# A decoder step: rows gathered without their norm, the factor gathered per slot, the last output product in two pieces, two subtractions on GpSimd

## The chip, the cores and the metric

One core of a Trainium2 chip runs the whole step. The metric is the device time of one launch in microseconds. The kernel before takes 429.27 us (median of 3 runs, 428.23 to 430.04).

## The reference

One layer of a decoder with 256 prompt tokens (two tiles of 128 rows, called 0 and 1) and 8 new tokens (tile 2, 8 rows), 1024 wide. What matters here comes after the attention:

```
hres = x + concat([att, conv_y]) @ w_out                 # output product
hn   = hres * rsqrt(mean(hres**2) + eps) * g_ffn         # second norm
lg, le = hn @ w_rg + b_rg, hn @ w_re + b_re              # 4 group logits, 32 expert logits
g    = argmax(lg);  two best experts inside group g, weights by softmax
h    = silu(hn @ w_gate[e]) * (hn @ w_up[e]) * gate
y    = hres + sum over the two experts of h @ w_down[e]; then a last norm
```

There are 32 experts with three 1 MB weights each in float32, so 96 MB of weights pass through the core whatever the tokens choose.

## The kernel before, in words

The work up to the expert groups is a list of named steps written out by hand (ORDER). Each engine (TensorE, VectorE, ScalarE, GpSimd) and SyncE's DMA queue takes its instructions in the order in which these steps issue them, so a step that waits holds back everything behind it on its engine.

For tile t the steps are: `o..` the output product with its add into yres; `H` per half of 512 columns the sum of squares on ScalarE, four transposes and their scaled copy xh; `l` the logits; `R` the norm's factor, whose power is taken on GpSimd (line 824); `L` the logits with the factor and bias; `N` the normed row rounded to the short float format, hn, on ScalarE (line 833); `O` what the rounding left, hlo, on VectorE (line 839). Products of the short format run faster, and hn and hlo together keep the precision. `ra` to `re` are the routing on VectorE (lines 872 to 912): best group, best and second expert, the choice matrix A, and the gates G. `rk` ranks a token among those of its expert by a matmul with A (lines 922, 923), `oh` makes of the rank the one-hot matrix Pg (line 938).

Tokens are gathered by matmuls with Pg: 32 slots for each of 4 experts, so 128 slots in a group (`g..`, line 949: hn and then hlo, for tiles 0, 2 and 1). The rows are copied out of PSUM (`gr`, line 958), transposed and scaled by g_ffn into xg (`gt`, lines 965, 966). `warm0` and `warm1` are matmuls whose result is not used (line 288). Then follow 8 groups: gate product pgt and hidden product pup (line 1085), silu (1146), the slot maps (1066 to 1075), the multiplication of the two (1155), the gather for the next group, the down product pyy (1099), and the combine back into yres (1116, 1190).

Weights go through a ring of 15 buffers of 1 MB and some free halves and quarters, filled from SP's queue in a fixed order. A load waits until the buffer's last reader is done. The buffers of the output weights take part in it: the last gate weight of group 1 waits for the last output product. Where the ring is full ahead of the groups, the next load waits for the gate product of group 0.

Of the kernel before, what the change touches and what calls it, by code (L numbers as in the profile page):

```python
# [19 lines left out]
D = 1024  # L20
NTOK = 256
NB = 8
H = 8
# [10 lines left out]
FILL = 4  # L34
# [52 lines left out]
def hymba_step(ctx: ExitStack, tc: tile.TileContext, x_prompt, x_sample, cache_k, cache_v, state_conv,  # L87
# [35 lines left out]
    with tc.manual_schedule():  # L123
# [626 lines left out]
        def out_mm(t, n, kk):  # L750
            if kk == 0:
                accs["o", t, n] = ps("py", "acc")
            po = accs["o", t, n]
            for c in range(4 * kk, 4 * kk + 4):
                T.matmul(po, lhsT=mixT[:, c, 128 * t:128 * t + 128], rhs=wo[n, c // 4][:, c % 4, :],  # L755
                         start=c == 0, stop=c == 7)
            if kk == 1:
                yv = yres[:, t, 512 * n:512 * n + 512]
                V.tensor_tensor(yv, yv, po, op=OP.add)
# [16 lines left out]
        for n in range(2):  # L776
            for t in range(2):
                for kk in range(2):
                    steps[f"o{t}{n}{kk}"] = lambda t=t, n=n, kk=kk: out_mm(t, n, kk)
            steps[f"z{n}"] = lambda n=n: out_quad(n)  # L780
            steps[f"y{n}"] = lambda n=n: out_sum(n)
# [6 lines left out]
        def norm2_half(t, hf):  # L788

            n = NR[t]  # L790
            if hf == 0:
# [5 lines left out]
                else:  # L797
                    hlo[t] = c4(f"hlo{t}", [128, 8, 128], F32R)
                ss2[t] = c1(f"ssb{t}", [128, 2])
                xh[t] = c4("xh", [128, 8, 128])  # L800
            y = yres[:n, t, 512 * hf:512 * hf + 512]
            S.activation(hlo[t][:n, 4 * hf:4 * hf + 4, :].rearrange("t c p -> t (c p)"), y, AF.Square,
                         accum_out=ss2[t][:n, hf:hf + 1])
            pt = ps("pt")
            pv_ = pt.rearrange("p (c n) -> p c n", c=4)
            for c in range(4):
                T.transpose(pv_[:, c, 0:n], y[:, 128 * c:128 * c + 128], ident[:n, :n])
            x = xh[t][:, 4 * hf:4 * hf + 4, 0:n]
            V.tensor_tensor(x, pv_[:, :, 0:n], gfT[:, 4 * hf:4 * hf + 4, None].to_broadcast([128, 4, n]), op=OP.mult)

        def norm2_log(t, hf):
            n = NR[t]
            if hf == 0:
                PL[t] = ps("pl", "acc")
            for c in range(4 * hf, 4 * hf + 4):
                T.matmul(PL[t][:n, 0:36], lhsT=xh[t][:, c, 0:n], rhs=wr[:, c, :], start=c == 0, stop=c == 7)

        def norm2_rs(t):
            n = NR[t]
            r = c1(f"rs{t}", [128, 1])  # L820
            rs2[t] = small(f"rsb{t}", [128, 1])
            V.tensor_tensor(r[:n], ss2[t][:n, 0:1], ss2[t][:n, 1:2], op=OP.add)
            V.tensor_scalar(r[:n], r[:n], 1.0 / D, EPS, op0=OP.mult, op1=OP.add)
            P.tensor_tensor(rs2[t][:n], r[:n], mhalf[:n], op=OP.pow)
# [6 lines left out]
        def norm2_hn(t):  # L831
            n = NR[t]
            S.activation(hn[t][:n].rearrange("t c p -> t p c"), yres[:n, t, :].rearrange("t (p c) -> t p c", c=8),
                         AF.Copy, scale=rs2[t][:n])

        def norm2_lo(t):

            n = NR[t]
            V.scalar_tensor_tensor(hlo[t][:n], yres[:n, t, :].rearrange("t (p c) -> t c p", c=8), rs2[t][:n],
                                   hn[t][:n].bitcast(F32), op0=OP.mult, op1=OP.subtract)  # L840

        for t in range(3):
            for hf in range(2):
                steps[f"H{t}{hf}"] = lambda t=t, hf=hf: norm2_half(t, hf)
                steps[f"l{t}{hf}"] = lambda t=t, hf=hf: norm2_log(t, hf)
            steps[f"R{t}"] = lambda t=t: norm2_rs(t)
            steps[f"L{t}"] = lambda t=t: norm2_L(t)
# [493 lines left out]
```

## Time and profile before

| what | us |
|---|---|
| runs before, median (lowest to highest) | 429.27 (428.23 to 430.04) |
| profiled execution, its own time | 429.14 |
| its span, first to last instruction | 427.1 |
| TensorE, VectorE, ScalarE, GpSimd busy | 377.5, 198.0, 90.6, 101.2 |
| data moved | 155.02 MB, mean 363 GB/s |

Busy shares are means over stages with different limits. The page cuts the span into 40 slices of 10.7 us; the timeline lists instructions with start, duration, engine, line, output and inputs, and in brackets what the engine had waited for. TensorE's clock has two levels; PEclk is the granted share of full speed.

### The profile page before, as it was taken

Reading aid. Unit: us, or ns where it says so; the run is one execution under the profiler, and the core shown is the slowest. Engines: PE = TensorE matmul, PEld = TensorE weight load, DVE = VectorE, ACT = ScalarE, POOL = GpSimd, SP = SyncE. Lnnn points to the kernel's source line nnn. Section 1 sums busy time; section 2 is a strip of 40 time slices with the busy share of each in tenths; the row PEclk is TensorE's granted clock in tenths of the full one; section 3 lists DMA queues with packets and bytes.
Section 4 is the critical chain, followed back from the end, with each engine's and each line's share of the span. In section 5 each row is a group of like instructions: output and inputs, shape, how many; then the busy total and the mean of one; then the engine's idle time right before and its main releaser. Section 6 shows DMA issues by size and latency. Waiting matters only on the chain.

```text
span 427.1 us, 6429 instructions
## 1 busy us (share of the span) xinstructions
PE 377.5 (88%) x2574; PEld 201.5 (47%) x2574; DVE 198.0 (46%) x383; ACT 90.6 (21%) x214; POOL 101.2 (24%) x101
## 2 busy tenths in 40 slices
PE   7899999899999999987989898979679689788981
PEld 6354355578775334345545444434334344343630
DVE  1257987899774024577424242405005106024045
ACT  4221223164330003332311121102002012011023
POOL 3627888978205001000000000000000000000022
PEclk9999999999999999985799999999969989799996
DMA  7999986869988999949299999999999999999953
GB/s 266 398 360 411 365 348 243 344 224 409 418 329 306 421 423 418 409 186 371 68 413 397 424 418 424 417 423 421 417 424 420 421 422 417 424 420 413 393 185 104
DMA packets 32979, 155.02 MB, mean 363 GB/s; under 512 B 3068, under 2 KB 5322, under 8 KB 17972
## 3 DMA queue, kind: packets, MB, share of 16 engines
q1 hardware_dynamic: 27328, 119.69, 70.1%
q0 software_dynamic: 5008, 33.80, 20.2%
q10 hardware_dynamic: 612, 1.11, 0.7%
q8 instruction: 21, 0.34, 0.3%
q14 instruction: 10, 0.08, 0.1%
HBM read 152.40 MB, written 2.20 MB: 362 GB/s over the span
## 4 chain that ended last, share of the span: by engine, by line
PE 38%; DMA 34%; DVE 12%; issue 8%; POOL 6%; ACT 1%; DVEq 0%; POOLq 0%; SPq 0%; ACTq 0%
DMA g<-in_w_gate_dram 10%; DMA u<-in_w_up_dram 9%; DMA d<-in_w_down_dram 9%; PE py L755 7%; DMA K<-in_cache_k_dram,idx 5%; PE pyy L1099 4%; PE pgt L1085 3%; PE pov L710 3%; DVE Sd L481 3%; PE accB L553 3%; PE px L949 3%; PE pup L1085 3%; POOL K L475 2%; POOL K L304 2%; PE warm L288 2%
## 5 line engine op out<-in xcount | busy, mean ns | idle before, releaser
L1085 PE MATMUL pup<-u,xg 128*32 128x256 f32 x472 | 40.6, 442 | 12.8 <-DMA u<-in_w_up_dram 12.7
L1062 POOL TENSOR_TENSOR PGw<-Pg,G 128x384 f32<-128x384 f32 x8 | 6.7, 834 | 177.1 <-DVE Pg L938 134.4
L1155 DVE TENSOR_TENSOR sh<-pup,sh 128x256 f32<-128x256 f32 x8 | 4.8, 603 | 91.3 <-PE pup L1085 84.2
L475 POOL TENSOR_TENSOR K<-K,qv 128x2048 f32<-128x2048 f32 x9 | 40.7, 4540 | 4.7 <-DMA K<-in_cache_k_dram,idx 3.1
L481 DVE TENSOR_REDUCE Sd<-K 128x32 f32<-128x2048 f32 x16 | 35.9, 2277 | 6.0 <-POOL K L475 5.9
L1085 PE MATMUL pgt<-g,xg 128*32 128x256 f32 x512 | 31.8, 384 | 3.6 <-DMA g<-in_w_gate_dram 3.6
L1085 PEld LDWEIGHTS pup<-u,xg 128*32 128x32 f32 x472 | 18.5, 126 | 31.1 <-DMA u<-in_w_up_dram 17.0
L949 PE MATMUL px<-hn,Pg 128*128 128x512 f32 (+1 forms) x48 | 23.0, 504 | 11.2 <-DVE Pg L938 11.2
L1099 PE MATMUL pyy<-d,hT 128*32 128x512 f32 (+1 forms) x272 | 30.7, 570 | 0.6 <-DVE hT L1176 0.6
L755 PE MATMUL py<-wo,mixT 128*128 128x512 f32 x64 | 30.2, 622 | 0.0
L1116 PE MATMUL pz<-Y,PT 128*128 128x512 f32 (+1 forms) x90 | 26.5, 421 | 0.7
L958 ACT COPY xr<-px 128x512 f32<-128x512 f32 x16 | 9.3, 587 | 83.1 <-PE px L949 83.1
L1190 DVE TENSOR_TENSOR yres<-yres,pz 128x512 f32<-128x512 f32 (+1 forms) x42 | 25.6, 670 | 0.0
L1085 PEld LDWEIGHTS pgt<-g,xg 128*32 128x32 f32 x512 | 16.3, 111 | 18.2 <-DMA g<-in_w_gate_dram 5.2
L1108 DVE SCALAR_TENSOR_TENSOR Y<-pyy,gsl,Y 128x512 fp32r<-128x512 f32 (+1 forms) x17 | 12.2, 719 | 25.3 <-ACT Y L1107 25.3
L1107 ACT ACTIVATE Y<-pyy,gsl 128x512 fp32r<-128x512 f32 (+1 forms) x17 | 11.3, 663 | 43.9 <-PE pyy L1099 43.9
L1116 PEld LDWEIGHTS pz<-Y,PT 128*128 128x128 f32 (+1 forms) x90 | 12.1, 154 | 17.9 <-ACT Y L1107 6.4
L949 PEld LDWEIGHTS px<-hn,Pg 128*128 128x128 f32 (+1 forms) x48 | 9.2, 195 | 23.8 <-DVE Pg L938 11.7
L304 POOL DMA_INDIRECT V<-in_cache_v_dram,idx x16 | 15.1, 947 | 22.1 <-PE pov L710 18.2
L755 PEld LDWEIGHTS py<-wo,mixT 128*128 128x128 f32 x64 | 12.3, 199 | 14.3 <-issue 14.1
L304 POOL DMA_INDIRECT K<-in_cache_k_dram,idx x16 | 15.6, 973 | 14.6 <-DMA K<-in_cache_k_dram,idx 7.8
L477 DVE TENSOR_TENSOR K<-K,qb 128x2048 f32<-128x2048 f32 x7 | 16.0, 2280 | 2.2 <-DMA K<-in_cache_k_dram,idx 2.2
(325 smaller groups left out, 595.2 us busy)
## 6 DMA issues: line engine op xcount, KB each, us to landing
g<-in_w_gate_dram SPq DMA_DIRECT2D x32, 1024.0 KB, 19.9
d<-in_w_down_dram SPq DMA_DIRECT2D x28, 1024.0 KB, 19.8
u<-in_w_up_dram SPq DMA_DIRECT2D x25, 1024.0 KB, 19.8
u<-in_w_up_dram SPq DMA_DIRECT2D x9, 512.0 KB, 14.5
wo<-in_w_out_dram SPq DMA_DIRECT2D x4, 1024.0 KB, 16.3
wk<-in_w_in_dram SPq DMA_DIRECT2D x2, 1024.0 KB
wv<-in_w_in_dram SPq DMA_DIRECT2D x2, 1024.0 KB, 32.2
wC<-in_w_in_dram SPq DMA_DIRECT2D x2, 1024.0 KB
```

The costliest lines, as they stand in the source:

```text
L304: P.indirect_dma_start(out=t, out_offset=None, in_=src, in_offset=bass.IndirectOffsetOnAxis(ap=idx[:, b, hh:hh + 1], axis=0))
L475: P.tensor_tensor(kslots[i], kslots[i], qv[:, None, :].to_broadcast([128, 4, 512]), op=OP.mult)
L477: V.tensor_tensor(kslots[i], kslots[i], qbs[b][:, None, :].to_broadcast([128, 4, 512]), op=OP.mult)
L481: V.tensor_reduce(Sd[:, b, 4 * hh:4 * hh + 4, :].rearrange("p i h -> p (i h)"), kslots[i].rearrange("p i (h d) -> p (i h) d", h=8), axis=A ...
L553: T.matmul(acc[:, 0:264], lhsT=W[pn, kk][:, c, 128 * m:128 * m + 128], rhs=xnT[:, cc, 0:264], start=cc == 0, stop=cc == 7)
L710: T.matmul(po[32 * j:32 * j + 32], lhsT=pvs[b // 4][:, b % 4, i, :], rhs=vslots[2 * b + i // 4][:, i % 4, :], start=s == 0, stop=s == 1, t ...
L755: T.matmul(po, lhsT=mixT[:, c, 128 * t:128 * t + 128], rhs=wo[n, c // 4][:, c % 4, :], start=c == 0, stop=c == 7)
L949: T.matmul(PX[grp, hf], lhsT=PgS[grp][:n, POS[t]].rearrange("p j s -> p (j s)"), rhs=(hn, hlo)[low][t][:n, 4 * hf:4 * hf + 4, :].rearrange ...
L1085: T.matmul(dst[32 * j:32 * j + 32, 0:256], lhsT=xg[:, c, 32 * j:32 * j + 32], rhs=w[:, 256 * k:256 * k + 256], start=c == 0, stop=c == 7, ...
L1099: T.matmul(py[32 * j:32 * j + 32, 0:w], lhsT=hT[:, c, 32 * j:32 * j + 32], rhs=dw[grp, j][:, 1024 * c + a:1024 * c + b], start=c == 0, sto ...
L1116: T.matmul(pz, lhsT=PTS[grp][:, 128 * t:128 * t + NR[t]], rhs=Y[:, i, 0:w], start=start and i == 0, stop=i == 1, skip_group_check=more)
L1190: V.tensor_tensor(yv, yv, pz[:m], op=OP.add)
```

## The change

- hn is now the rounded row without its norm, made per column piece right after the piece's add (in `H`), and hlo (`O`) the plain difference. Tile 1's second half is cut in two pieces of 256 columns. Tile 2's two `O` pieces are on GpSimd.
- The norm's factor is gathered per slot by three matmuls (`gather_rs`), and enters silu's scale and the multiplication of silu with pup. For group 0 this stands behind the gate products, for the other groups behind the gather of the rows.
- The last output product (tile 1, second half) is issued as two pieces of 256 columns with an add each.
- The routing takes the two best experts with MAX over 8 columns instead of two rounds of reductions.
- The part of tile 1's rank that needs only the other tiles is issued ahead (`rk1p`). Fillers are three times two matmuls of 256 columns instead of twice four of 128.
- The row copies of group 0 are shared by ScalarE and VectorE, as is the scaling into xg.
- In the groups the next group's Pg stands ahead of the multiplication of silu with pup.

```diff
-o001 V6 H00 G31 o011 V7 H01 X1 pe l00 o100 R0 l01 L0 ra0 rb0 rc0 o101 as rk0 N0 co rd0 z0 z1 y0 oh0 H10 y1 H20
-O0 H21 l20 R2 g00 re0 l21 L2 ra2 rb2 room o111 l10 N2 rc2 H11 O2 R1 g01 rk2 oh2 N1 rd2 l11 L1 ra1 rb1 rc1 g20 warm0 g21
-warm1 rk1 oh1 O1 g10h g11h re2 g10l gr0 g11l gr1 gt0 gt1 rd1 re1
+o001 V6 H00 G31 o011 V7 H01 X1 pe l00 o100 R0 l01 L0 ra0 rb0 O00 rc0 o101 as rk0 O01 co rd0 z0 z1 y0 oh0 H10 y1 H20
+H21 l20 R2 g00 O20 l21 O21 L2 ra2 rb2 room g01 o111 rc2 l10 O10 o112 H11 R1p H12 rk2 oh2 R1 O11 l11 l12 L1 ra1 rb1 rc1
+g20 warm0 g21 warm1 rk1p rk1 warm2 oh1 O12 rd2 g10h g11h re0 g10l ga0 g11l ga1 re2 gt0 gt1 rd1 re1
...
+        COLS = {0: ((0, 512), (512, 512)), 2: ((0, 512), (512, 512)), 1: ((0, 512), (512, 256), (768, 256))}
...
+            S.copy(hn[t][:n, :, p].rearrange("t c p -> t p c"), y.rearrange("t (p c) -> t p c", c=8))
+        def norm2_lo(t, k):
+            n = NR[t]
+            a, w = COLS[t][k]
+            p = slice(a // 8, (a + w) // 8)
+            (P if t == 2 else V).tensor_tensor(
+                hlo[t][:n, :, p], yres[:n, t, a:a + w].rearrange("t (p c) -> t c p", c=8),
+                hn[t][:n, :, p].bitcast(F32), op=OP.subtract)
...
+            V.scalar_tensor_tensor(r[:n, 1:2], ss2[t][:n, m:m + 1], 1.0 / D, r[:n, 0:1], op0=OP.mult, op1=OP.add)
+            P.tensor_tensor(rs2[t][:n], r[:n, 1:2], mhalf[:n], op=OP.pow)
...
+            V.max(e8, l8)
+            e1, e2 = e8[:, 0:1], e8[:, 1:2]
+            V.scalar_tensor_tensor(f, l8, e2, w8, op0=OP.is_ge, op1=OP.mult)
             yield
+            V.tensor_scalar(g8, l8, e2, 8.0, op0=OP.is_gt, op1=OP.mult)
+            V.tensor_tensor(f, f, g8, op=OP.add)
+            V.max(p8, f)
+            m1, m2 = p8[:, 0:1], p8[:, 1:2]
+            V.tensor_scalar(a8, f, m2, None, op0=OP.is_ge)
...
+            w = 256 if grp == 0 else 512
+            S.copy(rows_[:, 0:w], px[:, 0:w])
+            if w < 512:
+                V.tensor_copy(rows_[:, w:512], px[:, w:512])
+        def gather_rs(grp):
+            prs = ps("prs", "acc")
+            for t in range(3):
+                n = NR[t]
+                T.matmul(prs[:, 0:1], lhsT=fl(PgS[grp], t, n).bitcast(F32), rhs=rs2[t][:n], start=t == 0, stop=t == 2)
+            RSl[grp] = wp.tile([128, 1], F32, name="rsl", tag="rsl", bufs=2)
+            S.copy(RSl[grp], prs[:, 0:1])
...
+            m = 2 if grp == 0 else 4
+            V.tensor_tensor(XG[grp][:, 4 * hf:4 * hf + m, :], pt[:, 0:m, :],
+                            gffT[:, 4 * hf:4 * hf + m, None].to_broadcast([128, m, 128]), op=OP.mult)
+            for c in range(m, 4):
+                cc = 4 * hf + c
+                S.activation(XG[grp][:, cc, :], pt[:, c, :], AF.Copy, scale=gffT[:, cc:cc + 1])
...
             mm_exp(pgt, gw, grp)
+            if grp == 0:
+                gather_rs(0)
-            S.activation(sg, pgt[:, 0:256], AF.Silu)
+            S.activation(sg, pgt[:, 0:256], AF.Silu, scale=RSl[grp])
...
             mm_exp(pup, uw, grp)
+            if grp < LAST:
+                onehot(grp + 1)
+            V.scalar_tensor_tensor(hh_.rearrange("s c p -> s p c"), pup[:, 0:256].rearrange("s (p c) -> s p c", c=2),
+                                   RSl[grp], sg.rearrange("s (p c) -> s p c", c=2), op0=OP.mult, op1=OP.mult)
```

## Rows read from the trace of the kernel before

**Rows 1.** The page's slices: what all DMA engines moved, GB/s, per slice.
```profile
GB/s 266 398 360 411 365 348 243 344 224 409 418 329 306 421 423 418 409 186 371 68 413 397 424 418 424 417 423 421 417 424 420 421 422 417 424 420 413 393 185 104
```

**Rows 2.** The chain of waits: start, duration in us, what held the end.
```profile
271.41 19.81 DMA d<-in_w_down_dram
...
392.15 3.64 PE pgt L1085 x58
```

**Rows 3.** Windows: length, busy us per engine (instructions), granted clock, DMA share, GB/s.
```profile
185.50:190.00 4.50, 4.50 (x15) 2.27 (x14) 2.17 (x10) 0.90 (x1) 0.00 (x0) 0.81 0.02 7
190.50:203.80 13.30, 9.39 (x40) 6.70 (x39) 10.56 (x38) 2.68 (x6) 0.62 (x2) 0.63 0.95 352
194.00:207.50 13.50, 10.74 (x41) 7.33 (x45) 9.32 (x38) 3.29 (x6) 0.62 (x2) 0.50 0.71 266
204.00:212.00 8.00, 7.75 (x82) 4.49 (x80) 3.84 (x18) 3.51 (x8) 0.83 (x1) 0.77 0.01 3
226.00:228.00 2.00, 1.91 (x9) 0.94 (x7) 1.55 (x3) 0.41 (x1) 0.00 (x0) 1.00 0.77 283
```

**Rows 4.** Timeline of SP's queue: start, duration, issue of loads.
```profile
210.93 0.33 SPq L1017 DMA_DIRECT2D u<-in_w_up_dram  x1
...
212.30 13.62 SPq L1046 DMA_DIRECT2D d<-in_w_down_dram  x4
```

**Rows 5.** Timeline, all engines, from the last output product to the gate product.
```profile
184.41 5.08 PE L755 MATMUL py<-wo,mixT 128*128 128x512 f32 x8
...
189.53 0.69 DVE L759 TENSOR_TENSOR yres<-yres,py 128x512 f32<-128x512 f32 x1 [2.05 <-PE py L755]
...
191.92 2.04 DVE L839 SCALAR_TENSOR_TENSOR hn<-yres,rsb,hn 8x1024 fp32r<-8x1024 f32 x1
...
195.35 0.25 DVE L828 SCALAR_TENSOR_TENSOR L<-pl,rsb,biasb 128x36 f32<-128x36 f32 x1
...
198.53 2.08 PE L288 MATMUL warm<-ident 128*128 128x128 f32 x8
...
198.85 0.25 DVE L893 SCALAR_TENSOR_TENSOR A<-rcols 128x32 bf16<-128x32 f32 x1
...
201.17 0.29 DVE L938 TENSOR_TENSOR Pg<-rka,tab 128x128 fp32r<-128x128 f32 x1
...
206.87 4.04 PE L1085 MATMUL pgt<-g,xg 128*32 128x256 f32 x64
```

**Rows 6.** Prices: groups by shape (count, busy, mean ns), then single timeline rows.
```profile
L839 DVE SCALAR_TENSOR_TENSOR hlo<-yres,rsb,hn 128x1024 fp32r<-128x1024 f32 x2 | 4.1, 2074 | 0.0
...
L1176 DVE COPY hT<-pht 128x256 f32<-128x256 f32 x8 | 3.4, 425 | 25.0 <-PE pht L1174 25.0
...
183.78 0.55 POOL L824 TENSOR_TENSOR rsb<-rs,mhalf 8x1 f32<-8x1 f32 x1 [16.09 <-DVE rs L823]
...
196.81 0.16 DVE L874 TENSOR_REDUCE rcols<-rcols 128x1 f32<-128x8 f32 x1
...
200.70 0.21 PE L923 MATMUL prk<-A,trib 128*128 128x32 bf16 x1
...
203.36 0.15 DVE L905 RECIPROCAL rcols<-rcols 128x1 f32<-128x1 f32 x1
...
204.59 0.19 DVE L912 TENSOR_TENSOR G<-rcols 128x32 f32<-128x32 f32 x1
```

**Rows 7.** Timeline of GpSimd and VectorE during the attention's score products.
```profile
36.09 9.02 POOL L475 TENSOR_TENSOR K<-K,qv 128x2048 f32<-128x2048 f32 x2 [3.13 <-DMA K<-in_cache_k_dram,idx]
...
41.51 3.68 DVE L231 TENSOR_TENSOR rtmp<-qn,tab 128x64 f32<-128x64 f32 x1
45.12 0.21 DVE L232 TENSOR_TENSOR rtmp<-qn,tab 128x64 f32<-128x64 f32 x1
```

**Rows 8.** Timeline of TensorE in group 0: slot factors, first gather product of group 1.
```profile
211.37 0.91 PE L1073 MATMUL pgs<-ones__71,PGw 128*128 128x1 f32 x6
...
217.10 0.50 PE L949 MATMUL px<-hn,Pg 128*128 128x512 f32 x1 [1.23 <-DVE Pg L938]
```

More of the change, by code (lines that the diff above doesn't have):

```diff
@@ L33 @@
 WARM = 12
-FILL = 4
 KEEP = 12
@@ L753, in out_mm @@
             po = accs["o", t, n]
+            lo, w = (0, 512) if part is None else (256 * part, 256)
             for c in range(4 * kk, 4 * kk + 4):
-                T.matmul(po, lhsT=mixT[:, c, 128 * t:128 * t + 128], rhs=wo[n, c // 4][:, c % 4, :],
-                         start=c == 0, stop=c == 7)
+                T.matmul(po[:, lo:lo + w], lhsT=mixT[:, c, 128 * t:128 * t + 128],
+                         rhs=wo[n, c // 4][:, c % 4, lo:lo + w], start=c == 0, stop=c == 7,
+                         skip_group_check=part == 1)
             if kk == 1:
-                yv = yres[:, t, 512 * n:512 * n + 512]
-                V.tensor_tensor(yv, yv, po, op=OP.add)
+                yv = yres[:, t, 512 * n + lo:512 * n + lo + w]
+                V.tensor_tensor(yv, yv, po[:, lo:lo + w], op=OP.add)
         yq = {}
@@ L779, in hymba_step @@
                     steps[f"o{t}{n}{kk}"] = lambda t=t, n=n, kk=kk: out_mm(t, n, kk)
+            if n == 1:
+                for i in range(2):
+                    steps[f"o11{1 + i}"] = lambda i=i: out_mm(1, 1, 1, i)
             steps[f"z{n}"] = lambda n=n: out_quad(n)
@@ L814, in norm2_log, with norm2_pre @@
                 PL[t] = ps("pl", "acc")
-            for c in range(4 * hf, 4 * hf + 4):
+            for c in range(a // 128, (a + w) // 128):
                 T.matmul(PL[t][:n, 0:36], lhsT=xh[t][:, c, 0:n], rhs=wr[:, c, :], start=c == 0, stop=c == 7)
+        RT = {}
+        def norm2_pre(t):
+            n, m = NR[t], len(COLS[t]) - 1
+            r = RT[t] = c1(f"rs{t}", [128, 2])
+            if m == 1:
+                V.tensor_scalar(r[:n, 0:1], ss2[t][:n, 0:1], 1.0 / D, EPS, op0=OP.mult, op1=OP.add)
+            else:
+                V.tensor_tensor(r[:n, 1:2], ss2[t][:n, 0:1], ss2[t][:n, 1:2], op=OP.add)
+                V.tensor_scalar(r[:n, 0:1], r[:n, 1:2], 1.0 / D, EPS, op0=OP.mult, op1=OP.add)
@@ L864, in __call__ @@
                 return self.t[:, self.i - n:self.i]
-        RS = [Cols(f"rcols{t}", 80) for t in range(3)]
+        RS = [Cols(f"rcols{t}", 84) for t in range(3)]
         def route(t):
@@ L914, in route, with rank_before @@
             yield
-        def rank(t):
-            prk = ps("prk", "acc")
-            n, w = POS[t], prk[:, 0:32]
-            for k in range(n):
-                r = NR[ORD[k]]
-                T.matmul(w, lhsT=onesb[0:r, :], rhs=A[0:r, k, :], start=k == 0, stop=False)
+        PRK = {}
+        def rank_before(t):
+            PRK[t] = ps("prk", "acc")
+            for k in range(POS[t]):
+                r = NR[ORD[k]]
+                T.matmul(PRK[t][:, 0:32], lhsT=onesb[0:r, :], rhs=A[0:r, k, :], start=k == 0, stop=False)
+        def rank(t):
+            if t not in PRK:
+                rank_before(t)
+            n, w = POS[t], PRK[t][:, 0:32]
             T.matmul(w, lhsT=trib, rhs=A[:, n, :], start=n == 0, stop=True)
@@ L991, in hymba_step @@
             steps[f"rk{t}"] = lambda t=t: rank(t)
+            if t == 1:
+                steps["rk1p"] = lambda: rank_before(1)
             steps[f"oh{t}"] = lambda t=t: onehot(0, POS[t], 1)
@@ L998, in hymba_step, with fill @@
                 steps[f"g1{hf}" + "hl"[low]] = lambda hf=hf, low=low: gather_mm(0, hf, (1,), (low,))
-            steps[f"gr{hf}"] = lambda hf=hf: gather_rows(0, hf)
+            steps[f"ga{hf}"] = lambda hf=hf: gather_rows(0, hf)
             steps[f"gt{hf}"] = lambda hf=hf: gather_T(0, hf)
-        for i in range(2):
-            steps[f"warm{i}"] = lambda: keep_warm(FILL)
+        def fill(n):
+            w = ps("warm")
+            for _ in range(n):
+                T.matmul(w[:, 0:256], lhsT=ident, rhs=yres[:, 0, 0:256], start=True, stop=True)
+        for i in range(3):
+            steps[f"warm{i}"] = lambda: fill(2)
         SPLIT = {}
```

80 lines of the change are left out of this document (36 added, 44 removed).

## The prediction

> **What bounds the kernel now.** I read the slices of the page first. The transfer rate stands near 420 GB/s in nearly every slice from the twentieth on, and just ahead of that it sinks to 186, 371 and 68 [rows 1]: the expert weights are the load, and one hole lies before them. The chain of waits says the same: from 271.41 us it is one weight transfer behind the other, and only from 392.15 on TensorE work again [rows 2]. The windows show the hole closely: next to nothing is moved from 185.5 to 190 and from 204 to 212, with a refill from 190.5 to 203.8 between, and a small dip follows at 226 to 228 [rows 3]. Why: the ring of weight buffers is full. SP's queue shows the transfer of group 0's successor issued at 210.93, right behind the gate product of group 0, which runs from 206.87 for 4.04 us [rows 4, 5]. So the time is: when that product ends, plus a stream that is limited by bytes, plus a tail of 35 us. A microsecond taken off the path to the gate product is a microsecond off the end, as long as the hole is not used up. The refill starts when the last output product gives its weights back, and ends at 203.8; the gate product could end some 7 us earlier before the stream is unbroken.
>
> The path to it, in the timeline [rows 5]: the last output product ends near 189.5, its add runs at 189.53, tile 2's low part (2.04 us, VectorE) stands at 191.92 ahead of tile 1's norm, tile 1's logits come at 195.35, its choice A at 198.85, the ranks wait for a filler that began at 198.53, one-hot Pg at 201.17, first gate matmul at 206.87. TensorE's granted clock was half (1.2 GHz) from 194 to 207.5 [rows 3]; what TensorE did before it fell was transposes and matmuls of 36 columns, and then nothing for 2 us.
>
> **The change, part by part.** Times are of the profiled execution, 429.14 us (span 427.1, 2.0 around it); the median of the runs is 429.27, so I take the difference from 429.14.
>
> *Up to the last add.* Low parts are now cut to column pieces and need no norm: tile 0's leave the stretch at 181, two products of group 0 come ahead of the last output product (about 1 us), and the product itself comes in two halves of the same total work. The trace has it at 5.08 us with the clock half for its first part [rows 5]; and with less of that I put its end at about 189.3, where it was. But VectorE is then late, for this reason: tile 2's two low parts (8x512 each) go to GpSimd, right behind the norm of tile 2 (183.78 for 0.55 [rows 6]). GpSimd took 4.51 us per 2048 columns, so 1.13 us each [rows 7]; they run to about 186.6. In that time VectorE has tile 2's routing, and many of its operations take two operands from SBUF. What that does, the trace shows: while GpSimd ran a product from 36.09 to 45.11, a 128x64 VectorE operation lasted 3.68 us, to the moment GpSimd was done; the like one behind it took 0.21 [rows 7]. The Trainium skill has the rule (page "SBUF — State Buffer", section "Who interferes with whom"): VectorE with two SBUF inputs and a GpSimd instruction that reads SBUF exclude each other for the whole instruction; by it the two subtracts are not free although they are taken off VectorE, and this trace agrees (3.68 against 0.21 us). So I let the routing of tile 2 stand until 186.6. Then come what is left of its first two steps (four operations of 0.23, the mean found below, 0.95), the first half's add (0.35), the third step (five, 1.15) and the first low part of tile 1. A low part was 2.07 us for 1024 columns [rows 6]; less 0.15 for a small operation that is 1.88 ns per column, so 1.11 for 512 and 0.63 for 256. The second half's add starts at 190.1 instead of 189.53: 0.6 lost. Bounds: nothing lost, 0.3 won (no exclusion; 189.3); or, if a column costs GpSimd as much more on strided rows as I reckon for VectorE (1.9 us each), 1.5 more lost.
>
> *From that add to the logits.* Before, 189.53 to 195.35, 5.82 us. Now VectorE has: an add of 256 columns, 0.42 (a 128x256 copy [rows 6]); two xh pieces of 256 columns, 0.42 each; between them the two small operations of the norm's first part, 0.15 each; two for tile 2's ranks, 0.2 each; its one-hot, 0.3 [rows 5]; the norm's last, 0.15: 2.4. GpSimd's power, 0.55 [rows 6]. The next low part (0.63, two SBUF inputs) starts on VectorE just before it; I charge half of that as exclusion the other way, 0.3 (bounds 0 and 0.6). The logits start at 3.3 after the add: 2.5 won, of which 2.04 is tile 2's low part gone. TensorE's transposes and logits of the pieces and ScalarE's squares and rounded copies lie beside this: half of the old column count behind the last add, and 2.4 us for it.
>
> *Routing of tile 1.* Of ten dependent operations behind the eight logits seven stay, two of them a MAX over 8 columns that the trace does not show. The ten took 2.29 us (from 196.81 to the end of A, 199.10 [rows 5, 6]), 0.23 each; at that price 0.7 won. Bounds for a MAX: 0.15, the smallest operation, and 0.43, a 128x256 copy: 0.2 better to 0.4 worse for the two. I take the mean, since reductions over 8 columns lie there.
>
> *From A to Pg.* 2.32 us from start to start, because the rank matmul stood behind a 2.08 us filler [rows 5]. Now the part of the rank that needs no A of tile 1 is taken ahead, and at full clock the two fillers are over by 195: A 0.25, a hop 0.2, the matmul 0.2 [rows 6], the rank's operation 0.2: 0.9. Won 1.4, if the clock holds; the other end is the half-clock case below.
>
> *From Pg to the gate product.* 5.70 from start to start. I expect almost nothing here though the low part behind Pg shrinks from 2.07 to 0.63 us. On VectorE's queue there now stand between Pg and the first piece of xg: Pg 0.3, low part 0.5, five operations of tile 2's gates at 0.13 each, two full gate steps (203.36 to 204.78, 1.42 each [rows 6]), two halves of the row copies that ScalarE had alone (0.43, 0.35) and the half of xg, 0.42: 5.5. TensorE's four-product line with copies and transposes needs only about 4. Won 0.2. What was hidden behind the low part is now late itself. ScalarE's share of the copies lies beside it and is done earlier.
>
> *In the groups.* A factor gather is added per group: three matmuls of one column, like the six records of pgs, which held TensorE from 211.37 to 212.21, 0.84 (0.91 busy [rows 8]); group 0 gets two before its down product (its own and group 1's). Pg of the next group now stands on VectorE ahead of the multiplication behind pup (line 1155): TensorE waited 1.23 us for it until 217.10 [rows 8], and that goes. So the down product of group 0 ends 0.5 later behind its gate product than before. SP's queue waits for it with the fourth of the down loads (13.62 us over four issues [rows 4]), which is the dip at 226 to 228: it grows by 0.5. Bounds 0 and 1.7 (both gathers, no wait saved). In later groups TensorE is 0.4 shorter, and the stream hides it. Without that cover it would be a gain of 0.4 per group. Scaling silu and that multiplication by the factor are scalar operands of instructions that exist already; I count 0, at most 0.15 in the tail. On SP no load is added or changes its order; on GpSimd's queue only tile 1's power stands behind the two subtracts, at 192.5, long after 186.6.
>
> *Sum.* -0.6 + 2.5 + 0.7 + 1.4 + 0.2 - 0.5 = 3.7 us won. 429.14 - 3.7 = 425.4 us. The hole at 204 to 212 keeps some 4 us, so nothing of this is swallowed by the transfers.
>
> **The rivals.**
> *Half clock in the fillers.* TensorE works at 1.2 GHz through the new fillers. For it: the clock was half from 194 to 207.5 although fillers ran, and the thin work that came before it still stands there. Against it: before, TensorE then idled 2 us, and now wider fillers come at once. Price: from the one-hot of tile 2 (192.3) two products of 0.8 (0.50 at the full clock [rows 8]), two fillers of 2.08 and the early rank, 0.3: the rank at 198.3, not 196.7; a third filler of 2.08 ahead of the products, three products at 0.7 or more, copies, the gate step and xg: gate product at 205.7 instead of 202.6, so 3.1 of the 3.7 are gone. 428.5 us.
> *Exclusion does not bite.* The subtracts take 8 rows and the small operations slip between. The add comes at 189.3, the power is not held up, the dip stays: 0.8 + 0.3 + 0.4 more won, 423.9 us. Against it stand the 3.68 us of [rows 7].
> *GpSimd's subtracts are slow: slower than before.* The rows of y are read with a stride, which no GpSimd row of the trace shows. Both stand in sequence ahead of tile 2's routing, so each microsecond of one counts twice. At 1.9 us each it ends at 426.9; the gain is gone at 1.13 + 3.7/2 = 3.0 us each, and at 4.51, the longest GpSimd row, the time is 432. For it: the stride, and that the rest of the chain queues behind. Against it: half as many columns as the dearest VectorE case, which cost 2.07 for all 1024.
>
> **How the numbers follow.** My forecast with its own spread (424.3 to 426.9) 0.5; no exclusion and a better clock, below it, 0.17; half clock, 427 to 429.5, 0.2; slow subtracts beyond the break-even 0.08; the rest, 0.05, for something unseen in the buffers. Half a per cent (2.1 us, about what can be told from no change) makes the limits 427.1 and 431.4. Faster: 0.5 + 0.17 + some of the others 0.07 = 0.74. Slower: 0.08. Same: 0.18. The range: at the low end 423.9 less 0.4 for the gate product at full clock and 0.6 for the runs' scatter (428.23 to 430.04), 422.9; at the high end 428.8, the half-clock case and a little of that scatter.
>
> **What would show it.** Tile 2's routing standing still beside two GpSimd subtracts near 184 to 187, an operation of 0.2 stretched past 1 us; tile 1's logits 3.3 after the add; the rank within 0.5 us of A; VectorE busy without a gap from Pg to xg, with TensorE idle; the gate product starting at about 202.6; the transfers resuming at 208, then an unbroken rate but for a dip of about 1 us near 222. It is wrong if the first transfer behind the gate product moves by less than 2 us, if the rank waits for a filler again, or if the stream from there to the last gate weights is longer than the 181 us (210.93 to 392.15) of before.

## The result, and the profile after

The changed kernel takes 422.73 us (median of 4 runs, 421.82 to 423.49) beside 429.55 us for the kernel before (4 runs, 428.23 to 430.04): a ratio of 0.985 [0.981, 0.988]. Two later comparisons gave 0.983 [0.980, 0.986] and 0.985 [0.981, 0.988]. It is faster, as forecast, but by 6.8 us where 3.7 were forecast. The first median lies 0.2 us below the low end of the range (422.9), that of the second comparison (421.96) 0.9 below, that of the third (423.12) inside. So most of this section asks where the second half comes from.

The profiled execution took 423.49 us, its span is 421.8. First the stage up to the gate product, in the timeline of all engines (start, duration, engine, line, operation, and in brackets what the engine had waited for); it answers to [rows 5] and [rows 6].

```profile
182.67 3.00 POOL L827 TENSOR_TENSOR hn<-yres,hn 8x512 fp32r<-8x512 f32 x2
...
183.10 1.12 DVE L899 SCALAR_TENSOR_TENSOR rcols<-L,rcols,tab 128x4 f32<-128x4 f32 x1
...
184.45 1.27 DVE L906 SCALAR_TENSOR_TENSOR l<-rcols,L 128x32 f32<-128x32 f32 x1
...
186.34 0.41 DVE L760 TENSOR_TENSOR yres<-yres,py 128x256 f32<-128x256 f32 x1
...
186.81 1.99 PE L755 MATMUL py<-wo,mixT 128*128 128x256 f32 x8 [1.14 <-DVE yres L760]
...
188.85 0.42 DVE L760 TENSOR_TENSOR yres<-yres,py 128x256 f32<-128x256 f32 x1
...
191.83 0.25 DVE L862 SCALAR_TENSOR_TENSOR L<-pl,rsb,biasb 128x36 f32<-128x36 f32 x1 [0.40 <-POOL rsb L858]
...
192.87 1.13 PE L1063 MATMUL warm<-yres,ident 128*128 128x256 f32 x4
...
194.57 0.25 DVE L922 SCALAR_TENSOR_TENSOR A<-rcols 128x32 bf16<-128x32 f32 x1
194.88 0.18 PE L961 MATMUL prk<-A,trib 128*128 128x32 bf16 x1 [0.74 <-DVE A L922]
...
195.32 0.29 DVE L976 TENSOR_TENSOR Pg<-rka,tab 128x128 fp32r<-128x128 f32 x1
...
200.48 5.03 PE L1149 MATMUL pgt<-g,xg 128*32 128x256 f32 x64 [1.13 <-DVE xg L1018]
```

The reader is to see three things. GpSimd's two subtractions stand in one line of 3.00 us, and two small operations of VectorE with two SBUF operands stand still beside them (1.12 and 1.27 us; the same lines in tile 1's routing take 0.22 and 0.25). The second piece of the output product starts only when the first piece's add has read PSUM: a wait of 1.14 us. And the fillers run at the full clock (four in 1.13 us; at half they take 2.08, as a run below shows).

SP's queue, the answer to [rows 4], here with its first weight load of group 0's stage:

```profile
136.22 1.13 SPq L1110 DMA_DIRECT2D g<-in_w_gate_dram  x2
...
205.53 0.33 SPq L1081 DMA_DIRECT2D u<-in_w_up_dram  x1
...
206.90 13.93 SPq L1110 DMA_DIRECT2D d<-in_w_down_dram  x4
...
415.61 0.65 SPq L1308 DMA_DIRECT2D out_dram<-yo  x1
```

In the kernel before the first and the last of these lines read:

```profile
136.97 1.05 SPq L1046 DMA_DIRECT2D g<-in_w_gate_dram  x2
...
423.00 0.52 SPq L1241 DMA_DIRECT2D out_dram<-yo  x1
```

The chain of waits (start, duration, what held the end), for [rows 2], and the page's slices of GB/s, for [rows 1]:

```profile
256.05 19.57 DMA u<-in_w_up_dram
...
385.02 3.64 PE pgt L1149 x58
...
412.61 0.36 DVE yo L1306
```

```profile
GB/s 259 416 373 421 367 292 308 340 220 392 424 358 266 421 429 423 409 204 347 234 413 399 425 427 425 426 428 424 428 427 424 427 427 426 427 427 416 401 99 108
```

In the middle of the kernel the slices stand at 424 to 428, where they stood at 417 to 424. Over the fourteen slices from the 23rd on the mean is 426.3 against 420.9 GB/s. The instructions of the weight loads are the same in both.

With these lines the 5.65 us between the two profiled executions (429.14 and 423.49) can be split at fixed points:

| stretch | before | after | won |
|---|---|---|---|
| start to SP's first gate load of the ring | 136.97 | 136.22 | 0.75 |
| from there to the load behind the gate product | 73.96 | 69.31 | 4.65 |
| from that load to the last group's gate product | 181.22 | 179.49 | 1.73 |
| from there to the first yo | 27.59 | 27.59 | 0.00 |
| yo to the end of the last output's issue | 3.78 | 3.65 | 0.13 |
| from there to the span's end | 3.58 | 5.54 | -1.96 |
| around the span | 2.04 | 1.69 | 0.35 |

The first line cannot be put down to the work that was changed: that load is issued anywhere between 135.4 and 137.6 us in the fourteen profiles of this study. Below, starts within the stage are therefore counted from it. The second line is the change's own stage. The third and the sixth are in no part of the prediction.

### The profile page after: what moved, and what is told of

The parts are those of the page before. It is cut to its first block, busy times and chain, and to the rows that moved or that the text cites. A ratio compares the mean times of both kernels' runs of the same rounds, so it can differ in the third digit from the quotient of the medians.

```text
span 421.8 us, 6576 instructions
## 1 busy us (share of the span) xinstructions
PE 382.7 (91%) x2626; PEld 208.0 (49%) x2626; DVE 196.4 (47%) x384; ACT 92.0 (22%) x232; POOL 104.7 (25%) x103
## 4 chain that ended last, share of the span: by engine, by line
PE 42%; DMA 32%; DVE 13%; issue 7%; POOL 3%; ACT 1%; DVEq 0%; ACTq 0%; SPq 0%; POOLq 0%
DMA u<-in_w_up_dram 14%; DMA g<-in_w_gate_dram 9%; DMA d<-in_w_down_dram 8%; PE py L755 4%; PE pup L1149 4%; PE pov L709 3%; PE acck L238 3%; DVE Sd L480 3%; PE accB L552 3%; PE pgt L1149 3%; PE accq L238 3%; PE pyy L1163 3%; PE accv L238 2%; PE px L987 2%; POOL K L474 1%
## 5 line engine op out<-in xcount | busy, mean ns | idle before, releaser
L1149 PE MATMUL pup<-u,xg 128*32 128x256 f32 x472 | 42.9, 468 | 12.2 <-DMA u<-in_w_up_dram 12.2
L1223 DVE SCALAR_TENSOR_TENSOR sh<-pup,rsl,sh 128x256 f32<-128x256 f32 x8 | 5.3, 666 | 90.2 <-PE pup L1149 83.6
L755 PE MATMUL py<-wo,mixT 128*128 128x512 f32 (+1 forms) x72 | 29.0, 550 | 1.1 <-DVE yres L760 1.1
L998 ACT COPY xr<-px 128x512 f32<-128x512 f32 (+1 forms) x16 | 8.8, 557 | 68.0 <-PE px L987 68.0
L987 PE MATMUL px<-hn,Pg 128*128 128x512 f32 (+1 forms) x48 | 21.9, 480 | 0.1
L755 PEld LDWEIGHTS py<-wo,mixT 128*128 128x128 f32 x72 | 13.3, 190 | 13.5 <-issue 11.8
L1163 PEld LDWEIGHTS pyy<-d,hT 128*32 128x32 f32 x272 | 8.3, 111 | 17.7 <-issue 16.1
L238 PE MATMUL accq<-wq,xnT 128*128 128x512 f32 x32 | 16.3, 657 | 0.3 <-DVE xnT L221 0.3
```

Source lines behind the costliest of these rows:

```text
L238: T.matmul(acc, lhsT=xnT[:, cc, 128 * t:128 * t + 128], rhs=W[pn, kk][:, c, :], start=cc == 0, stop=cc == 7)
L755: T.matmul(po[:, lo:lo + w], lhsT=mixT[:, c, 128 * t:128 * t + 128], rhs=wo[n, c // 4][:, c % 4, lo:lo + w], start=c == 0, stop=c == 7, sk ...
L987: T.matmul(PX[grp, hf], lhsT=PgS[grp][:n, POS[t]].rearrange("p j s -> p (j s)"), rhs=(hn, hlo)[low][t][:n, 4 * hf:4 * hf + 4, :].rearrange ...
L1149: T.matmul(dst[32 * j:32 * j + 32, 0:256], lhsT=xg[:, c, 32 * j:32 * j + 32], rhs=w[:, 256 * k:256 * k + 256], start=c == 0, stop=c == 7, ...
L1163: T.matmul(py[32 * j:32 * j + 32, 0:w], lhsT=hT[:, c, 32 * j:32 * j + 32], rhs=dw[grp, j][:, 1024 * c + a:1024 * c + b], start=c == 0, sto ...
```

## The experiments

A number that recurs below is the "stretch": from SP's load behind group 0's gate product to the gate product of group 7, the third line of the table. The product's end of it is the start of the 58 of its 64 matmuls that wait for the last of its weights.

**The same two kernels again.** No edit.

> The changed kernel again, beside the kernel before on one chip. Its profile had the gate product of group 0 end 5.4 us earlier than before, the stream of weights behind it 1.7 us shorter (179.5 against 181.2 us) and the end of the program 1.8 us longer. Theory: only the first of these is the change, so it is 4.5 to 5.5 us faster than before. Rival: the shorter stream belongs to the change too (buffers come free earlier), then 6 to 7 us.

> The kernel before, profiled on the same chip. Theory: its stream, from the first load behind the gate product of group 0 to the first gate matmul of group 7, is within 0.6 us of the changed kernel's here. Rival: it stays at 181 us where the changed kernel has 179.5.

Measured: 421.96 us (421.66 to 422.98) beside 429.4, ratio 0.983 [0.980, 0.986]. The stretch was 179.44 us after (204.45 to 383.89) and 181.42 before (209.81 to 391.23). The 2 us are no scatter; they belong to the program. Group 0's gate product took 3.66 us here, not 5.03: in the first profile the granted clock was 0.50 of full speed from 200 to 203 us, in this one 1.00.

**Tile 2's subtractions back on VectorE.**

```diff
-            (P if t == 2 else V).tensor_tensor(
+            V.tensor_tensor(
```

> The changed kernel with tile 2's two low parts back on VectorE. Theory (exclusion): on GpSimd they took 1.5 us each and held two VectorE operations for 1.12 and 1.27 instead of 0.22 and 0.25 us, 1.9 in all; on VectorE they cost two subtractions of 1.07, of which 0.6 falls into a wait for GpSimd's power: the same or 0.4 us faster than the changed kernel, within 0.7. Rival (GpSimd took real work off the path): 1.5 to 2.1 us slower than the changed kernel.

Measured: 423.95 us (422.58 to 426.39), ratio 0.989 [0.986, 0.992]. That is 2.0 us more than the changed kernel beside it (421.96), which is what the rival had. The profile is of the fastest of the six runs; its span is 420.6 us, the same as that of the changed kernel beside it. VectorE's and SP's timelines:

```profile
182.77 2.10 DVE L827 TENSOR_TENSOR hn<-yres,hn 8x512 fp32r<-8x512 f32 x2
...
185.37 0.22 DVE L899 SCALAR_TENSOR_TENSOR rcols<-L,rcols,tab 128x4 f32<-128x4 f32 x1
...
185.82 0.25 DVE L906 SCALAR_TENSOR_TENSOR l<-rcols,L 128x32 f32<-128x32 f32 x1
...
189.20 0.42 DVE L760 TENSOR_TENSOR yres<-yres,py 128x256 f32<-128x256 f32 x1
```

```profile
204.53 0.33 SPq L1081 DMA_DIRECT2D u<-in_w_up_dram  x1
```

With GpSimd out of the way the two operations take 0.22 and 0.25 us: it was GpSimd that held them. VectorE does the work itself in 2.10 us, and the last add stands 52.2 us behind SP's first gate load, against 52.6 in three profiles of the changed kernel. In this profile the move to GpSimd took nothing off the path: what VectorE no longer did, it stood still for. The times do not agree with that. The other five runs took 423.53 to 426.39 us, at a mean granted clock of 0.947 to 0.954 where the profiled one had 0.961, and none of them has a profile. So the standing still is shown, what the move is worth in time is not: the times speak for the rival, and why stays open.

**Gates of tiles 0 and 2 moved out of the way.** The gate step of tile 0 ahead (behind `z1`), that of tile 2 behind both halves of xg.

```diff
-... co rd0 z0 z1 y0 oh0 ... oh1 O12 rd2 g10h g11h re0 g10l ga0 g11l ga1 re2 gt0 gt1 rd1 re1
+... co rd0 z0 z1 re0 y0 oh0 ... oh1 O12 g10h g11h g10l ga0 g11l ga1 gt0 gt1 rd2 re2 rd1 re1
```

> The changed kernel with the gate steps out of VectorE's queue between Pg and xg: re0 goes into VectorE's wait near 176, rd2 and re2 behind both xg. Theory (VectorE bounds this stretch, and TensorE's idling there lowers its clock for the gate product): the gate product starts near 198.0 instead of 200.5 and takes 3.6 to 4.0 us instead of 5.0; the slot maps then wait about 1 us for the gates; 2 to 3.5 us faster than the changed kernel. Rival (TensorE's line of products, copies and transposes bounds it, or the stream does): 0 to 0.5 us.

Measured: 422.0 us (420.93 to 425.23), ratio 0.985 [0.981, 0.990]: nothing won. The timeline, then windows (length, busy us per engine, granted clock, DMA share, GB/s):

```profile
197.85 3.66 PE L1149 MATMUL pgt<-g,xg 128*32 128x256 f32 x64
...
202.89 17.05 SPq L1110 DMA_DIRECT2D d<-in_w_down_dram  x4
...
204.23 0.91 PE L1137 MATMUL pgs<-ones__71,PGw 128*128 128x1 f32 x6 [1.35 <-POOL PGw L1126]
```

```profile
204.00:208.00 4.00, 3.77 (x46) 2.48 (x50) 0.00 (x0) 0.76 (x3) 1.00 (x2) 0.80 0.98 372
...
216.00:220.00 4.00, 4.00 (x35) 1.28 (x35) 1.44 (x2) 0.94 (x2) 0.00 (x0) 1.00 0.37 154
```

VectorE was what the gate product waited for: without the gate steps between Pg and xg it starts at 197.85, not at 200.78 as in the run of the changed kernel beside it; counted from SP's first gate load that is 1.9 us earlier. But then TensorE waits 1.35 us for the slot factors, its granted clock falls to 0.80 of full speed in the window, and from the start of the up product to that of the next product it takes 5.28 us instead of 3.59. The down product of group 0 ends where it ended, and SP holds the fourth down load for it, 17.05 us. That is longer than what is in flight lasts: the rate sinks to 154 GB/s at 216 to 220. The stretch is 182.67 us (201.52 to 384.19), 3.2 more than in the changed kernel beside it. The hole had been moved, not closed.

**Only the place of the buffers.** The diff has a line that the prediction passed over: the three tiles that hold the routing's small columns grew from 80 to 84 columns. With that the allocator puts every buffer behind them 96 bytes further up in each partition. The first buffer of the input weights begins at byte 40864 before and at 40960 after; the ring's 1 MB buffers, which share this region, begin at multiples of 4096 after, and 160 past a multiple of 256 before. The next two runs take this apart from everything else.

```diff
 # the kernel before
-        RS = [Cols(f"rcols{t}", 80) for t in range(3)]
+        RS = [Cols(f"rcols{t}", 84) for t in range(3)]
 # the kernel after
-        RS = [Cols(f"rcols{t}", 84) for t in range(3)]
+        RS = [Cols(f"rcols{t}", 92) for t in range(3)]
```

> The kernel before with one number changed: each of the three small tiles of routing columns has 84 columns in place of 80, as the changed kernel has them. Nothing reads the four new columns; all that moves is where the buffers behind these tiles lie in SBUF: by 96 bytes a partition, from 32 over a multiple of 64 to a multiple of 64. Theory, the place of the weights' buffers sets the rate of their stream: the stretch from the release of group 0's up weights to the gate product of group 7 takes 179.4 us as in the changed kernel and not 181.4, the transfers before it gain some tenths too, and the time is 2.0 to 3.0 us below the kernel before, near 427. Rival, the shorter stream comes from the changed order of the work (routing columns of the next group earlier, fewer waits in the stages): the stretch stays at 181.2 to 181.4 and the time within 0.6 us of the kernel before.

> The changed kernel with 92 columns in these tiles in place of 84, which puts the buffers back to 32 bytes over a multiple of 64; no instruction differs but in its addresses. Theory, the place of the buffers: the stretch from the release of the up weights to the gate product of group 7 goes from 179.4 back to 181.2 to 181.4 us and the time to 424 to 425.4, which is what the prediction had. Rival, the order of the work: 179.4 us, and 422.0.

Measured, kernel before with 84: 426.02 us (423.74 to 427.33), ratio 0.993 [0.990, 0.995]. Its slices, its load behind the gate product and its chain:

```profile
GB/s 260 418 370 419 329 320 330 303 220 368 422 387 235 421 426 426 414 244 375 64 399 402 421 429 424 428 425 427 426 425 428 425 428 425 427 426 421 408 181 105
```

```profile
210.02 0.33 SPq L1017 DMA_DIRECT2D u<-in_w_up_dram  x1
```

```profile
388.99 3.64 PE pgt L1085 x58
```

The stretch is 178.97 us, with the hole (64 in the 20th slice) untouched. Measured, kernel after with 92: 426.78 us (424.56 to 429.49), ratio 0.995 [0.992, 0.998]:

```profile
GB/s 238 397 354 416 363 346 250 375 223 363 413 394 249 423 421 419 412 224 341 288 383 426 422 419 422 419 422 420 422 422 422 419 419 422 419 426 407 383 110 107
```

```profile
205.57 0.33 SPq L1081 DMA_DIRECT2D u<-in_w_up_dram  x1
```

```profile
387.24 3.64 PE pgt L1149 x58
```

The stretch is 181.67. Both ways round, the place of the buffers switches the rate, 426 against 421 GB/s over the fourteen slices, with either order of the work. The second slice, in which the input weights are loaded, switches with it: 398 and 397 in the two programs whose buffers begin at 160 and 96 past a multiple of 256, 418 and 416 in the two at multiples of 4096. The work on the stage alone, without the lucky place, is worth 2.5 us by the times. The changed kernel was not timed on that chip; a run below has the same comparison beside it. All buffers behind the three tiles move together, so these runs do not part the weights' buffers from the others, but the fourteen slices hold little else than weight loads.

**Tile 2 without its second part.** Its rows are gathered by one float32 product; the two subtractions are gone.

```diff
-                hn[t] = c4(f"hn{t}", [128, 8, 128], F32R)
+                hn[t] = c4(f"hn{t}", [128, 8, 128], F32 if t == 2 else F32R)
...
+                if t == 2:
+                    T.matmul(PX[grp, hf], lhsT=PgS[grp][:8, POS[2]].rearrange("p j s -> p (j s)").bitcast(F32),
+                             rhs=hn[2][:8, 4 * hf:4 * hf + 4, :].rearrange("t c p -> t (c p)"), start=False, stop=False)
+                    continue
```

> The changed kernel, but tile 2's eight rows are gathered by one fp32 product from their own values instead of a product of first and second parts, so that its two subtractions on GpSimd, which hold two instructions of VectorE for about a microsecond each, are gone. Theory, these holds end on the path to the logits: the last add comes 1 us or more earlier, the gate product 1 to 2 us earlier, and the time falls 0.7 to 2. Rival, the holds lie in the shadow of the wait for the last output product: the gate product moves by less than 0.5 us and the time by less than 0.5.

Measured: 425.29 us (422.57 to 429.19), ratio 0.992 [0.988, 0.995], on a chip where the changed kernel itself was not timed; so no gain is shown. The profile is of its longest execution (429.19), and says what can happen, not how often:

```profile
192.29 0.25 DVE L919 SCALAR_TENSOR_TENSOR A<-rcols 128x32 bf16<-128x32 f32 x1
193.23 2.08 PE L1063 MATMUL warm<-yres,ident 128*128 128x256 f32 x4
...
195.40 0.21 PE L958 MATMUL prk<-A,trib 128*128 128x32 bf16 x1
```

The last add came 1.3 us earlier and A 1.5, counted from SP's first gate load: the two subtractions, and the standstill with them, had cost that. But the clock was at its lower level (four fillers in 2.08 us), and the rank's matmul, which stands behind fillers in TensorE's queue, came 3.1 us after A and not 0.31. This is the prediction's half-clock rival, in another kernel.

**Columns of the next group built late again.**

```diff
-            if grp < LAST:
-                onehot(grp + 1)
             hh_ = sh[:, 1, :].rearrange("s (c p) -> s c p", c=2)
             V.scalar_tensor_tensor(...)
             if grp < LAST:
+                onehot(grp + 1)
                 gather_x(grp + 1)
```

> The changed kernel with one step back where it was: in each group the columns for the next group's gather are built behind the product of gate and up, not ahead of it. Theory, in the middle of the kernel this work is hidden by the weights' stream: stretch of the stream 179.4 us as before and the time within 0.5 us of the changed kernel's. Rival, the shorter stream comes from this reordering: the stretch goes to 181.2 and the time up by 1.5 to 2.

Measured: 427.01 us (422.13 to 429.43), ratio 0.995 [0.991, 0.998]. That is 4 us more than the changed kernel has in its three comparisons, but with so wide a spread, and no run of the changed kernel beside it, the time alone decides nothing. In the profile (of the 422.13) SP's queue, and TensorE's weight loads at group 7's gate product, read:

```profile
205.03 15.30 SPq L1110 DMA_DIRECT2D d<-in_w_down_dram  x4
```

```profile
384.64 3.16 PEld L1149 LDWEIGHTS pgt<-g,xg 128*32 128x32 f32 x58 [0.42 <-DMA g<-in_w_gate_dram]
```

The stretch is 180.98 us (203.66 to 384.64), near the rival's 181.2: SP's four down loads take 15.30 us instead of 13.94, since the columns for group 1 now come on VectorE at 210.14, behind the up product, and TensorE waits 1.29 us for them ahead of the down product. The rate is 426 GB/s as after. So the order is worth 1.3 to 1.5 us of the stretch here, whether more in the time stays open, and it is not what switches the rate.

**The changed kernel as a yardstick, and buffers 64 bytes further.**

```diff
-        RS = [Cols(f"rcols{t}", 84) for t in range(3)]
+        RS = [Cols(f"rcols{t}", (84, 84, 100)[t]) for t in range(3)]
```

> The changed kernel once more, as the yardstick for the three runs beside it. Expected: 422 to 423 us, ratio to the kernel before 0.983 to 0.986, as in the first two comparisons; release of the up weights to the gate product of group 7 179.4 us. If the 427 us median of the kernel with the late columns came from that chip and not from its edit, the times here may reach 425 to 427 as well.

> The changed kernel with 100 columns in place of 84 in the last of the three tiles of routing columns: the weights' buffers move by 64 bytes a partition. As changed they begin at multiples of 4096 bytes; here they begin at 64 over such a multiple. Theory, what counts is whether a buffer begins on a multiple of 64: stretch of the stream 179.4 us and the time within 0.5 us of the changed kernel's. Rival, it takes a coarser multiple (128 bytes or more): the stretch goes to 181.2 to 181.7 as with 32 bytes, and the time up by 2 us.

Measured on one chip: the yardstick 423.12 us (421.21 to 424.42), ratio 0.985 [0.981, 0.988], with these lines, so a stretch of 179.71 us:

```profile
204.14 0.33 SPq L1081 DMA_DIRECT2D u<-in_w_up_dram  x1
```

```profile
383.85 3.64 PE pgt L1149 x58
```

With the buffers 64 bytes further 426.76 us (425.3 to 430.92), ratio 0.993 [0.991, 0.996]:

```profile
206.62 0.33 SPq L1081 DMA_DIRECT2D u<-in_w_up_dram  x1
```

```profile
388.31 3.64 PE pgt L1149 x58
```

The stretch is 181.69: the rival is right, a multiple of 64 is not enough. At 64 past a multiple of 4096 the load costs what it costs at 96 and at 160 past a multiple of 256 (420.4, 421.1 and 420.9 GB/s). The Trainium skill has a rule of this kind (page "DMA: Bandwidth & Descriptors", section "How a descriptor splits into AXI transactions"): a bus transaction of a transfer must start on a multiple of 256 bytes, and a piece that does not start there begins with a transaction from the boundary below, whose first bytes are fetched but not used. The page tells this of what is read; that it holds for the place in SBUF that is written, it does not say. The sign agrees with 426 against 421 GB/s; that this is the cause, and that 256 is the step, not 128 or more, no run here shows.

**Group 0 turned round, without and with the moved gates.** The up product directly behind the factor's gather, then the slot maps; the gather for group 1 behind the down product of group 0.

```diff
-            slot_maps(grp)
+            if grp > 0:
+                slot_maps(grp)
...
+            if grp == 0:
+                slot_maps(0)
...
             Ys = [gated(grp, down(grp, hT, 512 * n, 512 * n + 512), 512) for n in range(2)]
+            if grp == 0:
+                onehot(1)
+                gather_x(1)
+                for hf in range(2):
+                    gather_T(1, hf)
```

> The changed kernel with the order of group 0 alone turned: the up product directly behind the factor's gather, slot maps behind the up product, and the gather of group 1's rows behind group 0's down product. Nothing else moves. Theory, the stream's pause ends with group 0's down product, whose buffers the fourth of the down loads needs: that product comes 5 to 6 us earlier (pyy near 210.5 in place of 216), the four down loads are out by about 215 in place of 219.8, the gate product of group 7 comes 4 to 5 us earlier, and the time falls by 3.5 to 5, to 417 to 419. Rival, the loads' own rate is full by then or group 1's later gather costs as much: the loads are out earlier but the gate product of group 7 gains less than 1 us.

> The same, and the weights of tiles 0 and 2 reckoned in earlier and later places, as in the run that moved them (the gate product 2.9 us earlier there, the whole 0.3). Theory, that gain was given back at the down product: with the slot maps out of the way it shows, and this run is 2 to 3 us below the one with group 0's order alone, near 415. Rival, a fall of the granted clock behind the gate product takes it again, as it did there: within 0.7 us of the run with group 0's order alone.

Measured beside the yardstick: 423.77 us (421.24 to 427.34), ratio 0.987 [0.982, 0.992], and with the gates 423.38 us (420.77 to 424.56), 0.985 [0.980, 0.989]. Neither is faster. SP's queue in the first:

```profile
205.35 9.29 SPq L1110 DMA_DIRECT2D d<-in_w_down_dram  x4
214.73 14.06 SPq L1110 DMA_DIRECT2D g<-in_w_gate_dram  x4
```

The down product came 5 us earlier and the down loads were out at 214.64, not 219.47, just as the theory said. Yet the gate product of group 7 came at 383.62 against 383.85. The windows of the yardstick tell why:

```profile
204.00:208.00 4.00, 4.00 (x51) 3.03 (x51) 0.00 (x0) 2.25 (x5) 0.99 (x2) 1.00 0.66 183
208.00:212.00 4.00, 4.00 (x43) 2.06 (x35) 0.67 (x1) 0.28 (x1) 0.27 (x1) 1.00 1.02 423
212.00:216.00 4.00, 3.76 (x28) 2.64 (x31) 1.46 (x3) 1.05 (x3) 0.00 (x0) 1.00 1.01 426
216.00:220.00 4.00, 4.00 (x36) 1.33 (x29) 1.04 (x3) 1.37 (x2) 0.00 (x0) 1.00 0.95 395
220.00:226.00 6.00, 5.90 (x74) 2.99 (x72) 4.79 (x8) 0.00 (x0) 0.83 (x1) 1.00 0.94 378
```

While SP stood for 13.96 us, the transfers that had been issued filled the engines (share 1.02 and 1.01), and only at its end and just behind it is there a dent (395 and 378 GB/s; at 426 that is about 1 us lost). A wait of the issuing queue is not by itself a pause of the transfers. My theory for that run fell: the queue then stood 14.06 us for the next load instead, and about as little was lost by it (401 GB/s from 226 to 236). In the second run, counted from SP's first gate load, the load behind the gate product came 1.9 us earlier than in the yardstick and the gate product of group 7 0.8, and the median moved by no more than the runs scatter. There was little left to win: in the yardstick the transfers stand still only from about 203 to 205 us (29 and 0 GB/s), and in the second run they do not stop at all there (143 to 307 GB/s from 202 to 206). The prediction had left some 4 us of the hole. No version tried is measurably faster than the changed kernel.

## Why the prediction was right, and where not

Right were the direction, the mechanism and the size of the stage (4.2 us forecast up to the next load, 4.65 measured). Term by term, won in us, forecast and then measured in the profiled pair, starts counted from SP's first gate load:

| term | forecast | measured |
|---|---|---|
| up to the last add | -0.6 | -0.1 |
| add to logits | 2.5 | 2.8 |
| logits to A | 0.7 | 0.8 |
| A to Pg | 1.4 | 1.6 |
| Pg to gate product | 0.2 | 0.5 |
| gate product to the next load | 0 | -1.0 (+0.4 in two later profiles) |
| dip in group 0 | -0.5 | -0.3 in SP's queue (see below) |

- **Up to the last add.** The exclusion was real, with GpSimd dearer than the term had it (1.50 us a subtraction, not 1.13). The routing stood still until 185.7. That cost was offset, because tile 2's power came a microsecond earlier (182.05 against 183.78, 0.75 of that is the run's own), and what then set the add was a wait that the prediction did not have: TensorE's second piece waited 1.14 us until VectorE had read the first, which lies in the same PSUM bank. The Trainium skill has a rule that asks for it (page "PSUM — Partial Sum Buffer", section "PSUM bank collisions raise a hardware error"): a matmul and a read have to be kept apart by bank, not by address. The trace agrees, with the 1.14 us; whether two pieces in two banks would have gone free of it was not tried.
- **Routing.** The MAX over 8 columns takes 0.17 us, near the low bound of 0.15.
- **From Pg on.** VectorE is the bound, as the sum of its queue said: 4.84 us busy in the 5.2 us from 195.3 to 200.5, TensorE 2.97. The run with the moved gates shows the same by taking it away.
- **The half-clock rival** did not come here; it came in the run without tile 2's second part. The rival of slow subtractions needed 3.0 us each, and they took 1.5. Exclusion did bite.
- **The dip.** SP's four down loads took 13.93 us against 13.62, as forecast in sign. What that cost is hidden in the profiled pair by the changed rate, but programs with like buffers show it: with the buffers on multiples of 4096 the stretch is 179.44 to 179.71 us after and 178.97 before, off them 181.67 and 181.69 after and 181.22 and 181.42 before. So 0.3 to 0.7 us were lost, near the term's 0.5. The longer waits fit: 15.30 us gave a stretch of 180.98, 17.05 us one of 182.67.

The step that failed is "a stream that is limited by bytes, plus a tail of 35 us": the prediction took both as constants. The stream's bytes are the same, its rate is not: 1.73 us in the profiled pair, 3.2 us in the times when the place alone is changed in the kernel before (429.25 to 426.02), 3.6 when it is undone in the changed one (423.12 to 426.76). That the times show more than the stretch is not fully accounted for. The input weights' loads are faster too, and SP's first gate load is issued at 137.0 to 137.6 in the four profiles with the slow place and at 135.4 to 137.0 in nine of the ten others; but the tenth, the kernel before with moved buffers, has 137.4, so how much of it lies there stays open. With the place undone, the changed kernel is 2.5 to 2.7 us faster (ratios 0.995 [0.992, 0.998] and 0.993 [0.991, 0.996]) where 3.7, a ratio of 0.991, was forecast. Of the stage's 4 to 5 us, 0.3 to 0.7 went in the longer stretch and the rest at the program's end. From the last output's issue to the span's end it takes 3.58, 3.66 and 3.72 us in the three profiles with the old instructions, the one with moved buffers among them, and 4.47 to 5.98 in the eleven with the changed ones. In that time no engine starts an instruction that the trace shows, and beside the outputs only instruction code is transferred. What there takes longer was not tried, and stays open.

So the forecast of the work was near for a reason, and it did not see the other half of the gain, which came by luck. On the chip where all three programs were timed beside each other, 2.7 us came from the work that the change is about (429.43 to 426.76), and 3.6 from four added columns, by where they put the buffers (426.76 to 423.12).

## What to carry to other kernels

Read the diff for sizes too: a small tile that grows moves every buffer behind it, and a kernel that waits for a long stream of loads feels where its buffers begin; pad so that they begin on a large power of two (multiples of 4096 bytes did it here, 64 or 96 past one did not, larger steps were not tried), and try one program with only the pad before crediting anything else. Moving work to GpSimd beside VectorE operations with two SBUF inputs trades their time for standing still; in the profile VectorE won nothing by it, though the times of the version without the move were 2.0 us longer for a reason that was not found: a single profile, of the fastest run, does not overrule six times. A wait in the queue that issues loads matters only if what is in flight runs out first: look at the DMA share of the window, not at the length of the wait.

## What the runs showed of the hardware that was not expected

- Loads of 1 MB into 128 partitions ran at 426 GB/s into buffers that begin on multiples of 4096 bytes of the partition, and at 420 to 421 at 64, 96 and 160 bytes past a multiple of 256.
- GpSimd took 1.50 us for a subtraction of 8x512 with rows read in a stride of 8 elements, 2.9 ns a column; its contiguous products of 2048 columns took 2.2 ns [rows 7]. VectorE took 1.05 us for the same.
- The second of two column pieces of one product, in the same PSUM bank, started only when VectorE had read the first: 1.14 us of TensorE.
- The granted clock differs between executions of one program: the same gate product took 5.03 us in one profile (clock 0.50 from 200 to 203 us) and 3.66 in two others (1.00).
- SP's wait at the down loads cost nothing by its length alone: with 13.9 us of it the stretch was 179.4 to 179.7 us, with 15.3 us 181.0 and with 17.05 us 182.7, so in these profiles about all was lost that lay beyond 14 us.
